# Reordering the beginning of a one-core decoder kernel: loads, transposes, norm factors, constants and masks

## The chip, the cores and the metric

The kernel runs on one core of one Trainium2 chip. The metric is device time in microseconds (us) of one execution. Engines: PE is TensorE, DVE is VectorE, ACT is ScalarE, POOL is GpSimd, SP is SyncE, whose queue issues all DMAs here.

## The reference

One step of a two-layer decoder trunk over 576 tokens: 512 of a prompt and 64 of eight sampled sequences, 1024 features each. Layer A normalises the tokens, multiplies by a weight of 1024 x 8192 and runs a gated recurrence per head; layer B is sliding-window attention. The change touches only the way into layer A:

```python
def rms_norm(x, g):
    xf = x.astype(F32)
    y = xf * lax.rsqrt(jnp.mean(xf * xf, axis=-1, keepdims=True) + EPS)
    return (y * g.astype(F32)).astype(x.dtype)
...
def hgrn2_layer(x, s0, w_in, w_out, g_norm, g_onorm, lb):
    q, fz, i, gate = jnp.split(rms_norm(x, g_norm) @ w_in, 4, axis=-1)
```

## The kernel before

Activations lie with features on the 128 partitions: hT holds 8 feature blocks (k) of 576 tokens. Matrix products keep f32 accuracy by splitting each operand into a rounded part (hi) and the rest (lo) and adding three products: hi x hi, lo of x with hi of w, hi of x with lo of w. A product over all 576 tokens is two halves (j) of HN = 288 tokens, each with 24 steps: 8 k for each of the three terms (`product`, L222 to L236).

Where the tokens come from. `load_tokens` (L154) loads five tiles xt: four of 128 prompt tokens, one of 64 sample tokens. `arrive(i)` (L266 to L284) handles one tile: ScalarE squares it and sums over features (L272); TensorE transposes its eight blocks into two small PSUM tiles px (L276), which VectorE copies to hT (L277); ScalarE forms (mean + eps) to the power of minus one half by Ln and Exp (L278, L279); VectorE multiplies the identity by it (dg, L281); TensorE multiplies ones by dg (pr, L283), which spreads a token's factor over all partitions; ScalarE copies it to rall (L284). pr lies in the pool "m" of two large PSUM tiles that the products pf, pq, pi and pg use as well; px lies in the pool "x" of three.

`normed(j)` (L286 to L293) then makes the operands of one half: for each k, VectorE computes u = hT x gain x rall (L291), ScalarE copies it to xhi (L292), and VectorE, or GpSimd for k in LO_POOL = (1, 4, 7), subtracts to get xlo (L293). The gain is a column of vT, the transpose of a tile vecs that six small loads fill (L175, L298, L299). Half 0 needs tiles 0, 1 and a quarter of tile 2; half 1 needs tiles 2 to 4.

Order as written: loads of tiles 0 to 2, the six small loads, tiles 3 and 4, the sinks (L181); `arrive` of 0, 1, 2; vT; `normed(0)`; `arrive` of 3 and 4; `normed(1)`; the constants of the lower bound (L305 to L325); masks (L327 to L350); then layer A. There, `head_main(0)` (L578) forms pf (weights "a0_1"), pq ("a0_0"), pi ("a0_2") and pg ("a0_3"). Only pf of head 0 takes half 0 before half 1; its pq, pi and pg alternate between halves. `split_weights` (L195) loads a weight of 512 KB (raw, three buffers), casts it on ScalarE (whi, L200) and subtracts on VectorE (wlo, L204; two buffers each).

A scheduler reorders the program: each engine keeps one queue and works through it strictly in order, and the queue is built before the run from the program's order (earlier first), from priorities (`high_priority(offset)` lifts instructions by that many places, BOOST is 800, `early` 100), and from when the scheduler thinks an operand or a buffer is ready. `issue_after(ins)` puts the instructions traced inside it behind `ins` in the queue of the engine of `ins`, and binds no other engine.

## Time and profile before

| | us |
|---|---|
| median of 3 runs | 1169.92 (1169.79 to 1174.06) |
| the profiled execution, own time | 1169.39 |
| its span, first to last instruction | 1167.6 |
| TensorE busy in the span | 1111.7 (95%) |
| VectorE busy | 895.4 (77%) |
| ScalarE busy | 702.1 (60%) |
| GpSimd busy | 340.7 (29%) |

The span is the time between the first and the last instruction in the trace; 1.8 us of the execution's own time lie outside it. Busy time counts instructions of the engine itself; a wait in a queue shows as idle time, and the trace names what ended it. Times in the rows below count from the start of the span.

### The profile page before, as it was taken

Reading aid. Unit: us, or ns where it says so; the run is one execution under the profiler, and the core shown is the slowest. Engines: PE = TensorE matmul, PEld = TensorE weight load, DVE = VectorE, ACT = ScalarE, POOL = GpSimd, SP = SyncE. Lnnn points to the kernel's source line nnn. Section 1 sums busy time; section 2 is a strip of 40 time slices with the busy share of each in tenths; the row PEclk is TensorE's granted clock in tenths of the full one; section 3 lists DMA queues with packets and bytes.
Section 4 is the critical chain, followed back from the end, with each engine's and each line's share of the span. In section 5 each row is a group of like instructions: output and inputs, shape, how many; then the busy total and the mean of one; then the engine's idle time right before and its main releaser. Section 6 shows DMA issues by size and latency. Waiting matters only on the chain.

```text
span 1167.6 us, 27339 instructions
## 1 busy us (share of the span) xinstructions
PE 1111.7 (95%) x10937; PEld 1078.1 (92%) x10937; DVE 895.4 (77%) x2090; ACT 702.1 (60%) x1700; POOL 340.7 (29%) x311
## 2 busy tenths in 40 slices
PE   5999999999999999999999987999999999999997
PEld 5999999999999999999999987989989999999986
DVE  8898776489984597893897779567787778777686
ACT  6776764466662567772767455557655764765545
POOL 1122221112121131110122155444543453454430
PEclk8999999999999999999999998989999999999999
DMA  5332233232332523332232332211212213112102
GB/s 154 100 112 86 84 109 112 59 110 76 110 117 66 147 74 113 97 107 74 76 111 77 103 91 74 68 55 56 73 39 71 74 55 91 56 55 73 56 19 82
DMA packets 161097, 98.01 MB, mean 84 GB/s; under 512 B 3897, under 2 KB 157546, under 8 KB 160938
## 3 DMA queue, kind: packets, MB, share of 16 engines
q1 hardware_dynamic: 160970, 96.26, 28.0%
q8 instruction: 86, 1.41, 0.5%
q14 instruction: 41, 0.34, 0.1%
HBM read 84.06 MB, written 14.16 MB: 84 GB/s over the span
## 4 chain that ended last, share of the span: by engine, by line
PE 45%; DVE 11%; ACT 6%; issue 2%; POOL 1%; DVEq 0%; ACTq 0%; POOLq 0%
PE pbg L211 7%; PE po L211 7%; PE pbq L211 5%; PE po L228 4%; PE pg L228 3%; PE pf L228 3%; PE pi L228 3%; PE pq L228 2%; PE pkv L211 2%; PE sc L1098 2%; ACT P L1127 1%; PE pav L1181 1%; PE pz L211 1%; DVE QS L1289 1%; PE pa L797 1%
## 5 line engine op out<-in xcount | busy, mean ns | idle before, releaser
L606 POOL TENSOR_TENSOR Xl<-Xl 128x72 f32<-128x72 f32 x80 | 50.3, 659 | 205.9 <-DVE Xl L603 204.7
L638 POOL TENSOR_TENSOR sg<-sg,lg 128x576 f32<-128x576 f32 x16 | 26.3, 1642 | 278.4 <-ACT lg L571 278.4
L200 ACT CAST whi_a<-raw_a 128x1024 fp32r<-128x1024 f32 x64 | 67.1, 1049 | 63.4 <-PE po L228 30.8
L204 DVE TENSOR_TENSOR wlo_a<-raw_a,whi_a 128x1024 fp32r<-128x1024 f32 x64 | 81.8, 1282 | 25.0 <-issue 23.6
L1127 ACT ACTIVATE P<-P,st 128x192 f32<-128x192 f32 (+2 forms) x128 | 54.1, 424 | 68.4 <-DVE st L1122 68.4
L1136 POOL TENSOR_SCALAR P<-P,st 128x192 f32<-128x192 f32 (+1 forms) x64 | 48.6, 769 | 117.9 <-DVE st L1129 99.4
L438 DVE TENSOR_TENSOR hT<-hT,po 128x576 f32<-128x576 f32 x32 | 24.1, 754 | 49.6 <-PE po L228 49.3
L200 ACT CAST whi_o<-raw_o 128x1024 fp32r<-128x1024 f32 x30 | 31.4, 1047 | 30.8 <-PE po L228 25.6
L204 POOL TENSOR_TENSOR wlo_bg<-raw_bg,whi_bg 128x1024 fp32r<-128x1024 f32 x16 | 38.4, 2402 | 35.5 <-ACT whi_bg L200 30.0
L228 PE MATMUL po<-oh,whi_o 128*128 128x288 f32 x256 | 42.8, 302 | 4.4 <-ACT whi_o L200 1.9
L211 PE MATMUL po<-olb,whi_o 128*128 128x288 f32 x224 | 43.0, 306 | 3.8 <-DVE olb L1395 1.9
L211 PE MATMUL po<-ohb,whi_o 128*128 128x288 f32 x224 | 43.6, 311 | 2.4 <-DVE Qs L1294 1.7
L662 POOL TENSOR_TENSOR vb<-vst,bmask 128x512 fp32r<-128x512 f32 x32 | 36.7, 1168 | 26.7 <-DVE vst L658 13.8
L204 POOL TENSOR_TENSOR wlo_bq<-raw_bq,whi_bq 128x1024 fp32r<-128x1024 f32 x16 | 38.8, 2430 | 19.2 <-ACT whi_bq L200 19.1
L228 PEld LDWEIGHTS po<-oh,whi_o 128*128 128x128 f32 x256 | 35.9, 188 | 6.3 <-ACT whi_o L200 2.2
L211 PE MATMUL pbq<-xhi,whi_bq 128*128 128x256 f32 (+1 forms) x256 | 41.4, 305 | 0.0
L211 PE MATMUL po<-ohb,wlo_o 128*128 128x288 f32 x224 | 41.3, 301 | 0.0
L228 PE MATMUL po<-ol,whi_o 128*128 128x288 f32 x256 | 40.5, 294 | 0.0
L211 PE MATMUL pbg<-xhi,whi_bg 128*128 128x288 f32 x256 | 40.5, 300 | 0.0
L228 PE MATMUL po<-oh,wlo_o 128*128 128x288 f32 x256 | 40.4, 294 | 0.0
L211 PE MATMUL pbg<-xhi,wlo_bg 128*128 128x288 f32 x256 | 40.1, 299 | 0.0
L204 POOL TENSOR_TENSOR wlo_o<-raw_o,whi_o 128x1024 fp32r<-128x1024 f32 x14 | 33.6, 2399 | 22.0 <-ACT whi_o L200 20.3
(385 smaller groups left out, 3761.4 us busy)
## 6 DMA issues: line engine op xcount, KB each, us to landing
raw_a<-in_w_in_a_dram SPq DMA_DIRECT2D x64, 512.0 KB
S<-in_state_hgrn_dram SPq DMA_DIRECT2D x32, 256.0 KB
out_dram<-S SPq DMA_DIRECT2D x32, 256.0 KB
raw_o<-in_w_out_a_dram SPq DMA_DIRECT2D x16, 512.0 KB
raw_bq<-in_w_in_b_dram SPq DMA_DIRECT2D x16, 512.0 KB
raw_bg<-in_w_in_b_dram SPq DMA_DIRECT2D x16, 512.0 KB
raw_o<-in_w_out_b_dram SPq DMA_DIRECT2D x16, 512.0 KB
xt<-in_x_prompt_dram SPq DMA_DIRECT2D x4, 512.0 KB
```

Of the source, the lines that this page charges most:

```text
L200: act.copy(hi[:, :n], raw[:, :n])
L204: eng.tensor_tensor(lo[:, r], raw[:, r], hi[:, r].bitcast(F32), ALU.subtract)
L211: pe.matmul(pm[:, : c1 - c0], w[:, k * width + w0 : k * width + w0 + P], x(k)[i][:, c0:c1], start=n == 0, stop=n == len(terms) - 1,)
L228: pe.matmul(pm[:, j, :HN], w[:, k * width + c0 : k * width + c0 + P], x(k, j), start=n == 0 and k == 0, stop=n == 2 and k == nk - 1,)
L438: dve.tensor_add(h2, h2, ps2(pm))
L606: pool.tensor_tensor(X8[:, :, j : j + 1], X8[:, :, j : j + 1], X8[:, :, k : k + 1], ALU.add)
L638: (pool if SGP else dve).tensor_tensor(sg, sg, l, ALU.mult)
L662: pool.tensor_tensor(t, view(vst.bitcast(F32), [[0, 4], [1, P]], off=half * P), view(bmask, [[1, 4], [0, P]]), ALU.mult,)
L797: pe.matmul(pa[32 * j : 32 * j + ns, c, t0 : t0 + nt], keys[:, c * P + s0 : c * P + s0 + ns], queries[:, c * P + t0 : c * P + t0 + nt], st ...
L1098: pe.matmul(sc[:, hf, k0[hf] :], QS[pr][:, 2 * n + hf, :], kk[:, g, ks], start=q == 0, stop=q == 1)
L1127: act.activation(x, x, AF.Exp, bias=st[:, a : a + 1], accum_out=st[:, 8 + a : 9 + a])
L1136: (pool if e == "p" else dve).tensor_scalar(x, x, st[:, 8 + a : 9 + a], None, ALU.mult)
```

## The change

Loads (SP's queue): tiles 0 to 2, the gain norm_a into a tile of its own (vec_a), tiles 3 and 4, then the two weights a0_1 and a0_0, then the other five small loads and the sinks. Transposes: `arrive` keeps only transposes and copies to hT; squares, Ln, Exp, dg, pr and rall move to `factors`, with dg on GpSimd instead of VectorE and pr in the pool "x". Order: three tiles arrive, their factors, the gain's transpose, `normed(0)`; the copies of tiles 3 and 4 stand on VectorE behind the last xlo of half 0 (`first`), and the squares and so on of tiles 3 and 4 on ScalarE behind its last xhi (`first_high`). All xlo of `normed` are on VectorE. The casts of the first two weights get priority, right behind the third rall copy (`third`) and behind `first_high`. pq of head 0 takes half 0 before half 1, as pf does. On VectorE, all of head 0's first part stands behind `first`, and constants and masks stand behind the last xlo of half 1 (`second`).

```diff
-LO_POOL = (1, 4, 7)
...
     for i in range(3):
         load_tokens(i)
+    vec_a = stp.tile([KT, P], F32, name="vec_a")
+    sp.dma_start(vec_a, norm_a.rearrange("o (k p) -> (o k) p", p=P))
+    for i in range(3, 5):
+        load_tokens(i)
+
+    raws = {}
+    for part in (1, 0):
+        src = w_in_a[0, :, part * DI : part * DI + P].rearrange("(k p) c -> p k c", p=P)
+        raws[f"a0_{part}"] = wts.tile([P, 1024], F32, tag="raw", name=f"raw_a0_{part}", bufs=3)
+        sp.dma_start(raws[f"a0_{part}"].rearrange("p (a c) -> p a c", a=KT), src)
...
-        sp.dma_start(vecs[row : row + n, :], ap)
+        sp.dma_start(vecs[row - KT : row - KT + n, :], ap)
...
-    for i in range(3, 5):
-        load_tokens(i)
...
-        act.copy(hi[:, :n], raw[:, :n])
+        with ExitStack() as when:
+            if after:
+                when.enter_context(tc.issue_after(after))
+                when.enter_context(tc.high_priority(offset=BOOST))
+            act.copy(hi[:, :n], raw[:, :n])
...
-        junk = stp.tile([P, D], F32, tag="junk", name=f"junk{i}", bufs=2)
-        act.activation(junk[:n], xt, AF.Square, accum_out=q)
...
+    def factors(i):
+
+        n = P if i < 4 else LS
+        q = ssq[:n, i : i + 1]
+        junk = stp.tile([P, D], F32, tag="junk", name=f"junk{i}", bufs=2)
+        act.activation(junk[:n], xts[i][:n], AF.Square, accum_out=q)
         act.activation(q, q, AF.Ln, bias=eps_c[:n], scale=1.0 / D)
         act.activation(q, q, AF.Exp, scale=-0.5)
         dg = stp.tile([P, P], F32, tag="dg", name=f"dg{i}", bufs=2)
-        dve.tensor_scalar(dg[:n, :n], ident[:n, :n], q, None, ALU.mult)
-        pr = half(f"pr{i}")
+        pool.tensor_scalar(dg[:n, :n], ident[:n, :n], q, None, ALU.mult)
+        pr = misc(f"pr{i}")
         pe.matmul(pr[:, :n], ones[:n, :], dg[:n, :n], start=True, stop=True)
-        act.copy(rall[:, r], pr[:, :n])
+        return act.copy(rall[:, i * P : i * P + n], pr[:, :n]).ins
...
-            act.copy(xhi[:, k, r], u)
-            (pool if k in LO_POOL else dve).tensor_tensor(xlo[:, k, r], u, xhi[:, k, r].bitcast(F32), ALU.subtract)
+            high = act.copy(xhi[:, k, r], u)
+            low = dve.tensor_tensor(xlo[:, k, r], u, xhi[:, k, r].bitcast(F32), ALU.subtract)
+        return low.ins, high.ins
 
     for i in range(3):
         arrive(i)
+    for i in range(3):
+        third = factors(i)
+    pv = misc("pva")
+    pe.transpose(pv[:, :KT], vec_a, ident[:KT, :KT])
+    dve.tensor_copy(vT[:, :KT], pv[:, :KT])
+    first, first_high = normed(0)
+    with tc.issue_after(first):
+        for i in range(3, 5):
+            arrive(i)
+    with tc.issue_after(first_high):
+        for i in range(3, 5):
+            factors(i)
+    second, _ = normed(1)
     pv = misc("pv")
     pe.transpose(pv[:, :64], vecs, ident[:64, :64])
-    dve.tensor_copy(vT, pv[:, :64])
-    normed(0)
-    for i in range(3, 5):
-        arrive(i)
-    normed(1)
+    with tc.issue_after(second):
+        dve.tensor_copy(vT[:, KT:], pv[:, :64])
...
+        after = {(0, 1): third, (0, 0): first_high}.get((h, part))
...
-            yield from product(pq, *w, xview(xhi), xview(xlo))
+            yield from product(pq, *w, xview(xhi), xview(xlo), order=((0, 1),) if h else ((0,), (1,)))
...
-        for _ in head_main(0, st):
-            pass
+        with tc.issue_after(first):
+            for _ in head_main(0, st):
+                pass
...
-                make()
+                with tc.issue_after(second):
+                    make()
```

Left out: the same instructions for constants and masks (L305 to L350), now inside `with tc.issue_after(second):`, and the passing of `after` to `split_weights`.

## Rows read from the trace of the kernel before

**Rows 1.** The page, part 1: busy time of each engine over the whole span

```profile
PE 1111.7 (95%) x10937; PEld 1078.1 (92%) x10937; DVE 895.4 (77%) x2090; ACT 702.1 (60%) x1700; POOL 340.7 (29%) x311
```

**Rows 2.** Waits of TensorE, 0 to 60 us: total, times, longest

```profile
PE pr L283 <- DVE dg L281: 6.8, 1, 6.8
```

**Rows 3.** Stretches: length, busy time (count) by engine, PE clock, DMA share, GB/s

```profile
15.00:20.00 5.00, 0.00 (x1) 0.00 (x0) 5.00 (x11) 3.90 (x9) 1.94 (x2) 0.62 0.31 79
20.00:25.00 5.00, 3.17 (x11) 2.81 (x12) 5.00 (x13) 1.87 (x6) 0.84 (x1) 0.50 0.01 4
30.00:50.00 20.00, 20.00 (x156) 20.00 (x154) 15.67 (x38) 13.70 (x26) 3.81 (x6) 1.00 0.41 119
```

**Rows 4.** Timeline of TensorE, 4 to 38 us: start, length, line, tiles, count

```profile
4.32 1.94 PE L276 MATMUL px<-ident,xt 128*128 128x128 f32 x8 [4.32 <-DMA xt<-in_x_prompt_dram]
...
21.78 1.48 PE L283 MATMUL pr<-dg,ones 128*128 128x128 f32 x4 [6.78 <-DVE dg L281]
23.19 2.29 PE L228 MATMUL pf<-xhi,whi_a 128*128 128x288 f32 x8
...
35.57 2.24 PE L228 MATMUL pq<-xhi,wlo_a 128*128 128x288 f32 x16
37.65 0.55 PE L228 MATMUL pi<-xhi,whi_a 128*128 128x288 f32 x3
```

**Rows 5.** Timeline of VectorE, 14 to 31 us

```profile
14.40 1.80 DVE L291 SCALAR_TENSOR_TENSOR u<-hT,vT,rall 128x288 f32<-128x288 f32 x4
...
17.83 2.33 DVE L291 SCALAR_TENSOR_TENSOR u<-hT,vT,rall 128x288 f32<-128x288 f32 x4
20.09 0.81 DVE L293 TENSOR_TENSOR xlo<-u,xhi 128x288 fp32r<-128x288 f32 x2
...
23.60 1.37 DVE L291 SCALAR_TENSOR_TENSOR u<-hT,vT,rall 128x288 f32<-128x288 f32 x3
...
29.25 0.81 DVE L293 TENSOR_TENSOR xlo<-u,xhi 128x288 fp32r<-128x288 f32 x2
```

**Rows 6.** Timeline of ScalarE, 0 to 40 us

```profile
4.21 1.06 ACT L272 ACTIVATE junk<-xt 128x1024 f32<-128x1024 f32 x1 [2.21 <-DMA xt<-in_x_prompt_dram]
...
5.83 1.04 ACT L272 ACTIVATE junk<-xt 128x1024 f32<-128x1024 f32 x1
...
13.47 0.24 ACT L284 COPY rall<-pr 128x128 f32<-128x128 f32 x1
...
14.09 1.05 ACT L200 CAST whi_a<-raw_a 128x1024 fp32r<-128x1024 f32 x1
```

**Rows 7.** Timeline of SyncE's queue, 0 to 42 us

```profile
5.41 0.36 SPq L157 DMA_DIRECT2D xt<-in_x_prompt_dram  x1
...
8.65 15.46 SPq L198 DMA_DIRECT2D raw_a<-in_w_in_a_dram  x4
```

**Rows 8.** Instructions by line and form, 0 to 40 us: busy us, mean ns, idle before

```profile
L277 DVE COPY hT<-px 128x512 f32<-128x512 f32 x8 | 5.4, 684 | 0.6 <-PE px L276 0.6
L204 DVE TENSOR_TENSOR wlo_a<-raw_a,whi_a 128x1024 fp32r<-128x1024 f32 x4 | 5.3, 1326 | 0.0
...
L338 DVE TENSOR_TENSOR ge<-ti,si 128x128 f32<-128x128 int32 x1 | 0.3, 283 | 0.0
```

**Rows 9.** GpSimd's instructions by line and form, whole span

```profile
L1136 POOL TENSOR_SCALAR P<-P,st 128x128 f32<-128x128 f32 x16 | 10.0, 637 | 23.8 <-DVE st L1129 15.6 <-ACT pT L1227 4.5 <-ACT low L1184 3.7
```

**Rows 10.** Stretches in which TensorE's clock changes, columns as in Rows 3

```profile
21.78:26.20 4.42, 4.37 (x16) 3.98 (x17) 4.42 (x10) 1.88 (x6) 0.92 (x1) 0.50 0.21 61
852.80:855.80 3.00, 1.17 (x10) 1.13 (x10) 2.94 (x4) 0.00 (x0) 1.74 (x1) 1.00 0.02 7
855.90:859.10 3.20, 3.20 (x16) 3.20 (x15) 1.92 (x11) 1.36 (x7) 0.00 (x0) 0.50 0.54 154
```

**Rows 11.** Timeline of VectorE, 50 to 58 us

```profile
51.06 0.75 DVE L738 SCALAR_TENSOR_TENSOR KL<-KL,KQ 128x576 f32<-128x576 f32 x1
```

**Rows 12.** Timeline of TensorE from 57 us: first use of the first head's KL

```profile
57.27 0.22 PE L797 MATMUL pa<-KL 128*32 128x32 f32 x1
```

More of the change, by code (lines that the diff above doesn't have):

```diff
@@ L574, in weights_in @@
         def weights_in(h, part):
+            after = {(0, 1): third, (0, 0): first_high}.get((h, part))
             c = part * DI + h * P
[L576 removed]
+            return split_weights(w_in_a[0, :, c : c + P].rearrange("(k p) c -> p k c", p=P), f"a{h}_{part}", after=after)
         def head_main(h, st):
@@ L970, in yoco_kernel @@
             for make in {5: (prompt_mask,), 6: (sample_mask,), 7: (sink_rows,)}.get(h, ()):
-                make()
+                with tc.issue_after(second):
+                    make()
             st = nxt
```

97 lines of the change are left out of this document (48 added, 49 removed).

## The prediction

> **What bounds the kernel now.** I read the page's busy times first: TensorE works 95% of the span [rows 1], so a change at the beginning is worth what it moves TensorE's own work forward, as long as TensorE stays full behind it. The waits of TensorE come next: up to 60 us one wait stands out, 6.8 us for the diagonal dg at L281 [rows 2]. The stretches show the same hole: no work from 15 to 20 us, 3.17 of the next 5 us at a clock of 0.50, and from 30 to 50 us no idle time at all [rows 3]. So the beginning has one weak place, 15 to 26 us, and whatever is won is won when the product pi of head 0 starts, at 37.65 us [rows 4]; from there on TensorE runs full.
>
> Why the hole? TensorE's queue has the products pr of tiles 3 and 4 (21.78) in front of the first product pf (23.19) [rows 4]. Their dg stands in VectorE's queue behind all of half 0, whose subtraction ends at 20.09 + 0.81 = 20.90 [rows 5]. Half 0 began only at 14.40, because the third rall copy came at 13.47 [rows 6]. Weights are not the cause: the first cast of a weight ran at 14.09 [rows 6], nine us ahead of pf. Half 1 starts at 23.60 and ends at 30.06 (29.25 + 0.81) [rows 5].
>
> **The change part by part.** Paces first. VectorE makes an u in 0.45 us (4 in 1.80) and an xlo in 0.405 (2 in 0.81) [rows 5]: a k costs 0.855, a half of eight 6.84 us. A product step takes 0.13 us (16 from 35.57 to 37.65) [rows 4].
>
> Loads. xt3 was issued only at 5.41 and the first weight at 8.65, behind six small loads [rows 7]. Now three tokens, vec_a, two tokens and both weights go first, and five small loads and snk come behind them. The small ones feed vT's rest and sink_rows only, which now come after half 1: hidden. vec_a's 4 KB land beside xt2, while TensorE is still transposing. Earlier weights gain nothing alone, as the cast at 14.09 already lay ahead of its use; the cast of the first weight is now put right behind the third rall copy, and I take it that its data is there by then (the other case is a rival).
>
> Start of half 0. TensorE transposes from 4.32 at 0.24 us each (8 in 1.94) [rows 4]; 24 of them, now in front of the diagonals, end at 10.1. Three pr products follow; a pr cost 0.74 at the lower clock (1.48 for two) [rows 4], say 0.5 at the upper: 11.6. A rall copy takes 0.24 [rows 6] and a handoff 0.1: half 0 starts at 12.0 instead of 14.40. The vec_a transpose and its copy of eight columns lie beside that copy. VectorE's copies of hT (0.684 each [rows 8]) keep up, since the ten mask instructions and the diagonals no longer stand among them. dg on GpSimd has no row; the nearest, a TENSOR_SCALAR of 128x128, takes 0.637 [rows 9]; the lower end is VectorE's own 0.3 or less. Near the upper end only tile 2's counts, and ScalarE is done with that tile long before TensorE is.
>
> Half 0 on VectorE alone: 12.0 + 6.84 = 18.85. Before, GpSimd did three of the eight subtractions in each half (six, as LO_POOL has three k). That saves VectorE three times 0.405 = 1.2 us a half, but four u beside GpSimd took 2.33 instead of 1.80 [rows 5], which gives half of it back; so removing it costs about 0.7 us a half, which is already in the 6.84. The Trainium skill (GPSIMD Engine Reference, Specifications) says the two engines share SBUF interfaces and contend when a VectorE instruction has two SBUF inputs, as u and xlo have; by it alone the removal would look nearly free, and the trace agrees with 2.33 against 1.80.
>
> Start of half 1. This is the late link. ScalarE finishes the last xhi of half 0 near 18.4, and first_high holds everything for tiles 3 and 4 behind it. Then come the boosted cast of the second weight, 1.05 [rows 6], and two tiles at 1.62 each (4.21 to 5.83) [rows 6]: 22.7. Then dg 0.64, pr 0.5 to 0.74, copy 0.24, handoffs: rall is whole at 24.3. VectorE meanwhile does two copies of 0.684, two of half the columns at some 0.4, and two wlo of 1.33 [rows 8]: 18.85 + 2.2 + 2.7 = 23.7, so it waits 0.6 us. Half 1 runs from 24.3 to 31.15, **1.1 us later than the 30.06 of before**.
>
> TensorE. pr is now drawn from the small PSUM tiles, so pf need not stand behind pr3 and pr4: it starts at about 13.5, and the half-0 steps of pf and pq (48) are done before half 1 has delivered much. They have a wide cover, 13.5 to 26 us, even at the lower clock. What is left behind the last xhi of half 1 (30.7) is the xlo and wlo steps of two products: 32 x 0.13 = 4.2, to 34.9 against 37.65: 2.8 us won.
>
> The clock. Half 1 gives TensorE two xhi steps per 0.855 us, 0.26 us of work: 30% busy for over 4 us. No stretch of before is exactly that; the nearest is 852.8 to 855.8, with 1.17 of 3.00 us busy, after which the clock stood at 0.50 for 3.2 us, 1.2 of 2.4 GHz [rows 10]. The beginning of before cost 4.42 us at 0.50 [rows 10]. At that level a step takes twice as long: 3.2 us of it lose 1.6 us, 4.42 lose 2.2, and none lose 0. I take 1.6, by the nearest row. [...]
>
> Moved behind half 1: vT's copy, ten masks and the lower-bound constants, some 25 small instructions of VectorE. The widest takes 0.283 us [rows 8], so at most 7 us; most are far smaller, I take 4. They must lie beside pf's exponentials. VectorE was idle 20.00 - 15.67 = 4.3 us between 30 and 50 us [rows 3], and the first head's KL ended at 51.81 [rows 11], 5.4 us before TensorE used it [rows 12]. With pf 2 us later (at the lower clock) and pa 1.2 us earlier, 2.2 us of that are left: cost nothing, but not by much.
>
> Sum: 2.8 - 1.6 = **1.2 us won**. The profiled execution took 1169.39 (span 1167.6 and 1.8 around it), the median is 1169.92, 0.5 above; profile to profile 1168.2, as a median **1168.7 us**.
>
> **The rivals.**
> 1. Half 1 does not wait for its factors (ScalarE's squares of tiles 3 and 4 slip in earlier, or the cast of the second weight behind them). Then VectorE alone sets it: 18.85 + 2.2 + 6.84 = 27.9, or 29.2 with a wlo in between, and TensorE, dense at the full clock, ends 4.8 to 6.0 us earlier: 1164 to 1165. For it: VectorE has no idle time from 15 to 25 us today [rows 3]; against it: first_high is a hard order. 0.15.
> 2. Slower: TensorE takes the products as written, pf's half 1 before pq's half 0. It decides if the second weight's wlo, which the program names after half 1, is put behind it on VectorE. Then 64 steps stand behind the last xhi: 30.7 + 8.3 + 1.6 = 40.6, 3.0 later than 37.65: 1172.9. 0.13.
> 3. The loads do not come sooner. ScalarE's cast of the first weight now stands in front of all xhi copies, so a weight landing as late as 14.09 holds them: cast to 15.1, first xhi 15.55, while VectorE has filled its four u by 13.8 and stands for 1.75 us. All of it shifts: 2.8 - 1.75 - 1.6 = -0.55, 1170.5. Against it: the queue held the loads back at 5.41 and later, not the memory [rows 7]. 0.08.
>
> **How the numbers follow.** 0.64 is left for the forecast, which with the clock never falling gives 1167.1 and with 2.2 lost 1169.3. A measurement here tells about 0.5%, 5.9 us, from no change. The range runs from rival 1's early end with a little, 1163.5, to rival 2, 1172.9. Faster by over 0.5% needs the whole of rival 1 and some luck with the order of later work: 0.14. Slower by over 0.5% needs rival 2 with a further loss, such as pa waiting for KL: 0.06. Within 0.5%: 0.80.
>
> **What would show it.** Right: first u at 12, its last xlo near 19, pf at 13 to 14, a VectorE gap before half 1 at 24, pi at 35 to 37, a clock of 0.50 somewhere between 16 and 36 us, TensorE full from 37 on. Wrong: pi before 33 (rival 1), pi after 39 with pf's second half before pq's first (rival 2), ScalarE standing before whi for raw (rival 3), or a span that differs from the shift of pi by more than 2 us, which would mean that the later order changed.

## The result, and the profile after

The changed kernel takes 1174.29 us (median of 20 runs) against 1170.25 before (20 runs): the ratio is 1.0029, 95% interval 1.0020 to 1.0039. That is slower by some 3.4 us (the two medians lie 4.0 apart), within the 0.5% that counts as no change, and above the forecast's range. The profiled execution took 1172.9 with a span of 1171.1 (before 1169.39 and 1167.6), so the two profiles differ by 3.5 us, nearly as much, and can be read against each other.

The page's busy times after the change, to set beside [rows 1]: the engines' work is nearly what it was, TensorE 4 us more.

```profile
PE 1115.6 (95%) x10938; PEld 1080.0 (92%) x10938; DVE 896.2 (77%) x2092; ACT 702.0 (60%) x1700; POOL 340.4 (29%) x310
```

The waits of TensorE up to 70 us (us in total, times, longest), to set beside [rows 2]: the 6.8 us for dg are gone, and three waits stand at the start of pi and behind it that were not there.

```profile
PE pf L241 <- ACT xhi L309: 3.9, 5, 1.1
PE pf L241 <- DVE wlo_a L217: 1.8, 1, 1.8
PE pi L241 <- DVE KQ L592: 1.0, 1, 1.0
PE pa L827 <- issue: 0.8, 1, 0.8
```

**The beginning went as forecast up to half 1.** VectorE's timeline after (start, length, engine, line, operation, tile, count, and in brackets the idle time ahead and what ended it), against [rows 5]:

```profile
11.71 1.38 DVE L308 SCALAR_TENSOR_TENSOR u<-hT,vT,rall 128x288 f32<-128x288 f32 x3
17.63 0.89 DVE L310 TENSOR_TENSOR xlo<-u,xhi 128x288 fp32r<-128x288 f32 x2
21.60 2.35 DVE L217 TENSOR_TENSOR wlo_a<-raw_a,whi_a 128x1024 fp32r<-128x1024 f32 x2
25.53 1.38 DVE L308 SCALAR_TENSOR_TENSOR u<-hT,vT,rall 128x288 f32<-128x288 f32 x3 [1.57 <-ACT rall L301]
31.34 0.89 DVE L310 TENSOR_TENSOR xlo<-u,xhi 128x288 fp32r<-128x288 f32 x2
```

Half 0 starts at 11.71 (forecast 12.0, before 14.40) and ends at 17.63 + 0.89 = 18.52 (forecast 18.85, before 20.90). Half 1 starts at 25.53 (forecast 24.3, before 23.60) and ends at 32.23 (forecast 31.15, before 30.06): 2.2 us later than before, where 1.1 was forecast. These are the ends on VectorE; GpSimd's last xlo of before ended at 30.74. VectorE waited 1.57 us for rall. ScalarE's timeline, GpSimd's, and the view of the tile dg from 20 to 26 us (shortest, median and longest ns) say why:

```profile
21.34 0.33 ACT L296 ACTIVATE ssq<-ssq 128x1 f32<-128x1 f32 x2
24.92 0.57 ACT L301 COPY rall<-pr 128x128 f32<-128x128 f32 x2 [3.25 <-PE pr L300]
```

```profile
10.06 0.60 POOL L298 TENSOR_SCALAR dg<-ident,ssq 128x128 f32<-128x128 f32 x1 [1.47 <-PE pr L300]
21.62 3.14 POOL L298 TENSOR_SCALAR dg<-ident,ssq 128x128 f32<-128x128 f32 x2 [10.96 <-ACT ssq L296]
```

```profile
L298 POOL TENSOR_SCALAR dg<-ident,ssq x2: 437/1580/2722, 21.6 to 24.3; 128x128 f32<-128x128 f32 x1, 64x64 f32<-64x64 f32 x1
```

The factors were ready at 21.67, a us sooner than forecast. But tile 3's dg took 2.72 us on GpSimd, from 21.62 to 24.34, beside VectorE's two wlo that run from 21.60 to 23.95: it ended 0.4 us after them. The dg at 10.06, with no such neighbour, took 0.60, and tile 4's, at 24.3, took 0.44. The Trainium skill (SBUF — State Buffer, Who interferes with whom) calls the pair of ports that VectorE and GpSimd share an exclusive lock, held for a whole instruction, which a VectorE operation with two inputs in SBUF contends for with a GpSimd one that reads SBUF. The trace agrees: 2.72 us against 0.60, and the end just behind wlo's, though dg was held over two instructions and not one.

TensorE's timeline after, against [rows 4] and [rows 12]:

```profile
13.13 1.06 PE L241 MATMUL pf<-xhi,whi_a 128*128 128x288 f32 x3 [0.34 <-ACT xhi L309]
35.36 1.22 PE L241 MATMUL pq<-xhi,wlo_a 128*128 128x288 f32 x8
37.58 0.64 PE L241 MATMUL pi<-xhi,whi_a 128*128 128x288 f32 x3 [1.00 <-DVE KQ L592]
57.30 2.38 PE L241 MATMUL pf<-xhi,wlo_a 128*128 128x288 f32 x16 [1.80 <-DVE wlo_a L217]
64.71 0.19 PE L827 MATMUL pa<-G 128*16 128x16 f32 x1 [0.83 <-issue]
```

pf starts ten us sooner (13.13 against 23.19), and the last step of pq ends at 36.58, 1.2 us before the 37.81 of before: the forecast's gain, to the tenth. There it stops. pi waits a whole us for KQ (VectorE, L592), which reads pq out of one of the two large PSUM tiles and so frees it, and starts at 37.58 against 37.65. VectorE's rows of these reads, after and then before (lf at L625 and L595 is the last to read pf):

```profile
36.68 0.76 DVE L592 TENSOR_SCALAR KQ<-pq 128x576 f32<-128x576 f32 x1 [0.28 <-DMA S<-in_state_hgrn_dram]
39.21 0.75 DVE L625 SCALAR_TENSOR_TENSOR lf<-pf,lf 128x576 f32<-128x576 f32 x1
```

```profile
36.03 0.76 DVE L595 SCALAR_TENSOR_TENSOR lf<-pf,lf 128x576 f32<-128x576 f32 x1
37.85 0.76 DVE L563 TENSOR_SCALAR KQ<-pq 128x576 f32<-128x576 f32 x1 [1.05 <-PE pq L228]
```

Before, pi started ahead of KQ, in the tile that lf had left at 36.79. After, it started ahead of lf, in the tile of pq itself. It could not be free sooner: KQ began 0.1 us behind pq's last step, when VectorE had been idle for 0.28 us, so VectorE was not late for it. The order of pq brings this about. In two halves, pq ends 2.3 us behind pf (34.32 to 36.58); alternating, as before, it ended 5.3 us behind it (32.48 to 37.81), time enough to read pf out.

Then head 1's pf stands for 1.80 us behind its wlo, and a product pa pauses for 0.83 with no operand late that the trace names. In VectorE's queue after:

```profile
53.16 0.75 DVE L592 TENSOR_SCALAR sg<-pg 128x576 f32<-128x576 f32 x1
54.89 1.22 DVE L805 TENSOR_TENSOR KQ<-KQ,E 128x1024 f32<-128x1024 f32 x1
56.03 1.22 DVE L217 TENSOR_TENSOR wlo_a<-raw_a,whi_a 128x1024 fp32r<-128x1024 f32 x1
```

And in the kernel before, VectorE's timeline, then TensorE's, over the same instructions:

```profile
53.40 1.22 DVE L204 TENSOR_TENSOR wlo_a<-raw_a,whi_a 128x1024 fp32r<-128x1024 f32 x1
54.54 0.75 DVE L563 TENSOR_SCALAR sg<-pg 128x576 f32<-128x576 f32 x1
55.20 1.21 DVE L775 TENSOR_TENSOR KQ<-KQ,E 128x1024 f32<-128x1024 f32 x1
```

```profile
55.03 2.29 PE L228 MATMUL pf<-xhi,wlo_a 128*128 128x288 f32 x16
```

Before, wlo stood ahead of sg and KQ, was done at 54.62 and was used at 55.03: 0.4 us of slack. After, the queue has sg and KQ first, and wlo is done at 57.25. Of the 2.63 us by which it starts later, 1.8 are the places of sg and KQ (0.66 and 1.14 us of the queue), and 0.8 is VectorE's own lateness.

**Where the 3.5 us are.** For every profile of this study I took three numbers against the profile of before: how much later pi of head 0 starts, how long TensorE waits behind it up to head 1's pg, and how much later that pg starts. The first two add up to the third within half a us where the granted clock held in that stretch; in e10, e13, e14 and e15 it did not, and the steps themselves took 1.5 to 4.2 us more. After: -0.07 + 1.8 + 0.8 = 2.5, and pg is 2.47 late. The other us comes at 268 to 276 us, where TensorE's stretches (busy time of PE, PEld, DVE, ACT, POOL; PEclk, DMA share, GB/s) after and then before are:

```profile
268.00:272.00 4.00, 2.64 (x30) 1.85 (x29) 3.91 (x8) 3.91 (x8) 0.00 (x0) 1.00 0.00 0
272.00:276.00 4.00, 3.67 (x17) 3.67 (x18) 3.88 (x9) 3.85 (x18) 0.00 (x0) 0.57 0.50 147
```

```profile
268.00:272.00 4.00, 2.96 (x20) 2.58 (x21) 3.88 (x8) 3.94 (x15) 0.00 (x0) 1.00 0.42 125
272.00:276.00 4.00, 4.00 (x31) 3.92 (x30) 4.00 (x10) 3.79 (x13) 0.00 (x0) 1.00 0.10 27
```

In both kernels TensorE has gaps at 268; only after does the granted clock then fall to 0.57, and 16 steps of pi take 3.58 us instead of 2.37 (after, then before):

```profile
272.78 3.58 PE L241 MATMUL pi<-xlo,whi_a 128*128 128x288 f32 x16
```

```profile
270.17 2.37 PE L228 MATMUL pi<-xlo,whi_a 128*128 128x288 f32 x16
```

The lateness grows there from 2.42 to 3.80 us; by the end of the kernel it is 3.5. Other profiles have such a dip at other places or not at all.

### The profile page after: what moved, and what is told of

It reads as the page before. It is cut to its first block, busy times and chain, and to the rows that moved or that the text cites. A ratio compares the mean times of both kernels' runs of the same rounds, so it can differ in the third digit from the quotient of the medians.

```text
span 1171.1 us, 27350 instructions
## 1 busy us (share of the span) xinstructions
PE 1115.6 (95%) x10938; PEld 1080.0 (92%) x10938; DVE 896.2 (77%) x2092; ACT 702.0 (60%) x1700; POOL 340.4 (29%) x310
## 4 chain that ended last, share of the span: by engine, by line
PE 46%; DVE 11%; ACT 5%; issue 2%; POOL 1%; DVEq 0%; ACTq 0%; POOLq 0%
PE pbg L224 7%; PE po L224 6%; PE pbq L224 5%; PE po L241 4%; PE pg L241 3%; PE pf L241 3%; PE pi L241 3%; PE pq L241 2%; PE pkv L224 2%; PE sc L1130 2%; ACT P L1159 1%; PE pav L1213 1%; PE pz L224 1%; PE pa L827 1%; DVE QS L1321 1%
## 5 line engine op out<-in xcount | busy, mean ns | idle before, releaser
L241 PE MATMUL pf<-xhi,whi_a 128*128 128x288 f32 x256 | 41.5, 306 | 4.0 <-ACT xhi L309 3.9
L241 PEld LDWEIGHTS pf<-xhi,whi_a 128*128 128x128 f32 x256 | 35.4, 189 | 6.4 <-ACT xhi L309 5.6
L241 PE MATMUL pf<-xhi,wlo_a 128*128 128x288 f32 x256 | 37.6, 298 | 3.7 <-DVE wlo_a L217 3.7
```

Source lines behind the costliest of these rows:

```text
L241: pe.matmul(pm[:, j, :HN], w[:, k * width + c0 : k * width + c0 + P], x(k, j), start=n == 0 and k == 0, stop=n == 2 and k == nk - 1,)
```

## The experiments

The letters in the expectations: A, the place of that one wlo in VectorE's queue; B, masks and constants behind half 1; C, half 1's end, carried along VectorE's chain to head 0's attention copy; D, the forecast's rule that only the start of pi counts; E, a loss made only by the order behind 50 us, which pq's order in halves upsets; F and H, the amount of VectorE's work; G, late factors passed on through pf. A shift is against the profile of before; a ratio is to the runs of before on the same chip, 1.0029 being that of the change. Executions differ at the front even where nothing there was edited: half 1 ends 0.73 us late in e13 and 0.69 in e16, whose edits lie behind it. A shift of less than a us tells little.

**e1: lift the late wlo (from after).**

```diff
-                eng.tensor_tensor(lo[:, r], raw[:, r], ...
+                with tc.high_priority(offset=BOOST if name == "a1_1" else 0):
+                    eng.tensor_tensor(lo[:, r], raw[:, r], ...
```

> The changed kernel, with only the subtraction for head 1's first weight (wlo of a1_1) lifted in VectorE's queue, so that it stands some fifteen places earlier. Theory A (the late place of that one subtraction costs TensorE its 1.8 us wait at 55.5 us): the wait goes, product pi of head 1 starts near 69 instead of 70.8, and the time falls by 1.5 to 2.5 us. Rival B (VectorE simply has too much work between 32 and 57 us, the masks and constants among it): the same work in another order, so the wait moves to the products pa of head 0 and the time stays within 0.7 us.

1175.73 us, 1.0042 (1.0029 to 1.0055). The lifted wlo ran at 45.57 and the wait for it is gone. But kd, Qz and the wlo behind them now ran beside GpSimd's vb and sg (57.40 to 61.47) and took 1.26, 1.06 and 2.48 us instead of 0.42, 0.22 and 1.22; TensorE waited further on, for kt and for S:

```profile
PE pu L874 <- ACT kt L861: 1.6, 1, 1.6
```

A's fall of 1.5 to 2.5 us did not come. As the new place of that wlo cost VectorE some 2.9 us elsewhere, the run does not tell what the wait alone was worth.

**e2: masks back ahead of half 1 (from after).** The lower-bound constants stay behind it.

```diff
-    with tc.issue_after(second):
-        m_ge, m_8 = ...
+    m_ge, m_8 = ...
...
-                with tc.issue_after(second):
-                    make()
+                make()
```

> The changed kernel, with the ten mask instructions and the sinks no longer bound behind half 1; they run among the first copies of hT, as before the change. Rival B (moved work crowds VectorE): 2 us of VectorE work leave the stretch from 32 to 57 us, the 1.8 us wait for wlo of head 1 goes, and the time falls by about 2 us. Theory A (order, not amount): the wait for that wlo stays, because the subtraction still stands behind KQ, and the time changes by less than 1 us.

1177.58 us, 1.0058 (1.0045 to 1.0071): worse. One of the mask instructions, at the head of VectorE's queue, needed an iota that stood on GpSimd behind two dg, and VectorE stood 2.76 us for it (e10 shows such a row). That held the hT copies, so that the first u came at 14.66 and half 1 ended 5.1 us late. pi starts 2.90 late, the waits for wlo and at pa are there as well (1.7 and 1.8), sum 6.4, pg 6.28. The wait for wlo stays though the masks are gone from behind half 1, which speaks against B. The time decides nothing, as the held copies made half 1 late.

**e3: factors of tiles 3 and 4 not held behind the last xhi (from after).**

```diff
-    with tc.issue_after(first_high):
-        for i in range(3, 5):
-            factors(i)
+    for i in range(3, 5):
+        factors(i)
```

> The changed kernel, with the squares and factors of tiles 3 and 4 not bound behind the last xhi of half 0. Theory C (the late rall holds half 1, and with it pf, back): half 1 starts near 23 instead of 25.5, pf's last step comes 2 us earlier than 34.3, pi at 35.5 to 36.5 instead of 37.6, and the time falls by 1 to 2 us if the rest keeps its order. Rival D (pi's start is set by when a PSUM tile comes free): half 1 is earlier, pi is not, and the time stays within 0.7 us.

1172.92 us, 1.0017 (1.0005 to 1.0029). The edit did not bring half 1 forward: on ScalarE the squares of tiles 3 and 4 (9.28 to 12.57) now stood ahead of the rall copies, so half 0 began at 14.24. Half 1 ends 3.2 us late and pi starts 2.87 late, but nothing waits behind it, and pg is 2.68 late, as in after. A kernel that is late at pi ends no later than one that is on time there: with pi so late, the wlo that stands behind sg and KQ here too is in time.

**e4: head 0's pq alternating between halves, as before (from after).**

```diff
-            yield from product(pq, ..., order=((0, 1),) if h else ((0,), (1,)))
+            yield from product(pq, ...)
```

> The changed kernel, with head 0's pq alternating between the halves as before the change. Rival E (the split of pq into halves upsets the order behind it): the time falls by 2 to 3 us. Theory A: in VectorE's queue head 1's wlo stands ahead of sg and KQ again, as before the change, so the 1.8 us wait goes; but 16 more steps stand behind the last xhi of half 1, so pi starts about 1 us later (38.5) and the time falls by 0.5 to 1.5 us.

1171.54 us, 1.0009 (0.9999 to 1.0019). By the ratios that is 2.3 us below after, the 2 to 3 us that E had forecast. All three waits of after are gone, and in VectorE's queue wlo is ahead of sg (and of KQ, at 57.62) again, as A and E had it:

```profile
55.81 1.22 DVE L217 TENSOR_TENSOR wlo_a<-raw_a,whi_a 128x1024 fp32r<-128x1024 f32 x1
56.95 0.75 DVE L592 TENSOR_SCALAR sg<-pg 128x576 f32<-128x576 f32 x1
```

pi is 2.88 late and pg 2.42, with no wait between them. The profiled execution took 1173.83 us, 2.3 above the median of the run: ScalarE stood 0.91 us for the first weight, and half 1 ended 4.1 us late, 1.9 later than in after. Even so pg is no later than in after. So the 1.2 us that the order in halves won at pq was lost again behind it.

**e5: pr from the small PSUM tiles alone (from before).**

```diff
-        pr = half(f"pr{i}")
+        pr = misc(f"pr{i}")
```

> Edit of the kernel before, one line: pr of the five tiles is drawn from the small PSUM tiles, as the change does, so that pf of head 0 need not stand behind pr of tiles 3 and 4 on TensorE. Nothing of VectorE, ScalarE or GpSimd moves. Theory C (VectorE's queue sets the time from the end of half 1, 30.1 us in the profile of before, to head 0's copy att at 62.1 us): pf starts some 5 us earlier (near 17 instead of 23.2), half 1 still ends within 0.5 us of 30.1, att's copy comes within 0.7 us of 62.1, and the time is that of before within 1 us. Rival D (TensorE is full from 30 us on, so an earlier product start is worth its whole length, the rule of the forecast): pi of head 0 starts 2 to 4 us earlier and the time falls by as much.

1170.16 us, 0.9995 (0.9985 to 1.0004). pf starts at 17.06 instead of 23.19, and pi 0.22 later than before, with half 1 ending 1.27 later (31.33). The one wait of 6.8 us that I had put first was worth nothing that shows in the time: xlo and wlo steps wait for half 1 in any case.

**e6: VectorE held up ahead of half 1 (from before),** by four fills of a tile that nothing reads.

```diff
-    normed(0)
+    first = normed(0)
+    idle = stp.tile([P, 576], F32, name="idle")
+    with tc.issue_after(first):
+        with tc.high_priority(offset=BOOST):
+            for i in range(4):
+                dve.memset(idle, float(i))
```

> Edit of the kernel before: four memsets of a 128x576 tile that nobody reads, about 0.5 us each by the widest copies of this size, some 2.2 us together, stand on VectorE behind the last subtraction of half 0 and ahead of half 1. Everything else is as before. Theory C: half 1 ends 2.2 us later, near 32.3 (where the change puts it), head 0's copy att comes 2.2 us later, near 64.2, and the time rises by 2 us or a little more, to 1172 to 1174. Rival D (VectorE has 4.3 us idle between 30 and 50 us and 5.4 us of slack at KL, as the forecast priced it): att's copy moves by less than 1 us, and the time stays within 1 us of before, or follows pi's start alone.

1171.89 us, 1.0011 (1.0002 to 1.0020). Half 1 ends 1.75 late, pi starts 2.38 and pg 1.84 late: a late half 1 costs, in before as well, here some 1.3 us.

**e7: dg of tiles 3 and 4 on VectorE (from after).**

```diff
-        pool.tensor_scalar(dg[:n, :n], ...
+        (dve if i > 2 else pool).tensor_scalar(dg[:n, :n], ...
```

> Edit of the changed kernel: the diagonals dg of tiles 3 and 4 are made on VectorE, as in the kernel before, and no longer on GpSimd, where the two took 1.5 us each beside VectorE's wlo. Theory C: dg takes 0.3 us, rall is whole some 1.2 us sooner if dg's place in VectorE's queue is ahead of wlo (near 23.7), half 1 ends near 31 instead of 32.2, and the time is 1 to 1.3 us below the changed kernel's, between it and before; if dg stands behind the two wlo, nothing is won. Rival E (the loss lies only in the order behind 50 us, whenever half 1 ends): half 1 ends earlier and the time stays the changed kernel's within 0.7 us.

1173.49 us, 1.0025 (1.0015 to 1.0034): the same as after. The two dg are short now (0.44 for both), but without a lift they stood behind a wlo in VectorE's queue, at 23.47, behind an hT copy that came at 22.00; half 1 began at 26.20. To be held by wlo in the queue or beside it on GpSimd came to the same.

**e8: factors of tiles 3 and 4 between the xhi copies of half 0, and e4 (from after).**

```diff
+            if not j and k in (2, 5):
+                with tc.issue_after(high.ins):
+                    with tc.high_priority(offset=BOOST):
+                        factors(3 + k // 5)
```

> Edit of the changed kernel: the factors of tiles 3 and 4 are put on ScalarE between the xhi copies of half 0 (behind its third and its sixth), no longer behind the last one, and head 0's pq takes its steps in the two halves alternately, as in the kernel before. Theory C: half 0 runs at most 2 us longer on VectorE (its u wait for ScalarE's copies), half 1 follows behind the hT copies without a wait for rall and ends between 29 and 30.5 us, 2 to 3 us sooner than in the changed kernel; head 0's copy att comes as much earlier as half 1 ends, and the time is at or up to 1 us below before, 1169 to 1171.5. Rival F (the masks and constants that were moved behind half 1 are what costs, about 2 us of VectorE wherever half 1 ends): half 1 ends sooner, and att's copy and the time stay 1.5 us or more above before.

1174.70 us, 1.0032 (1.0018 to 1.0046). The factors were early, but the hT copies of tiles 3 and 4 then waited 3.4 us for their transposes behind TensorE's steps; half 1 ran from 26.94 to 34.53, and pi is 2.82 late. Tiles 3 and 4 need both.

**e9: three xlo of each half on GpSimd again (from after).**

```diff
-            low = dve.tensor_tensor(xlo[:, k, r], ...
+            low = (pool if k in (1, 4, 7) else dve).tensor_tensor(xlo[:, k, r], ...
```

> Edit of the changed kernel: three of the eight xlo subtractions of each half go back to GpSimd (k = 1, 4, 7), as in the kernel before. It takes 6 x 0.405 = 2.4 us of instructions off VectorE, and gives about half of it back, as u beside GpSimd is slower. Theory G (half 1's start is held by its factors, and behind half 1 the chain through pf, ka and the scan sets the time, not the volume of VectorE's work): half 0 ends at most 1 us sooner, half 1 still starts within 0.5 us of 25.5 and ends within 0.5 us of 32.2, and the time is the changed kernel's within 1 us. Rival H (VectorE's volume of work ahead of head 0's att copy, some 53.5 us in every run, sets that copy; the moved subtractions are what costs): att's copy and the time come 1.5 to 2.4 us sooner.

1174.69 us, 1.0031 (1.0019 to 1.0043). Half 1 ends at 33.01 on VectorE, later than 32.23, but the first weight came 1.2 us later too (ScalarE stood 1.27 us for it, 0.19 in after). H gets no support: fewer instructions for VectorE gained nothing, as three u beside GpSimd take 1.90 us instead of 1.38.

**e10: fills to GpSimd behind its last dg, masks first (from after).**

```diff
-    with tc.issue_after(second):
-        m_ge, m_8 = ...
+    m_ge, m_8 = ...
...
-        dve.memset(rmask, 1.0)
+        with tc.issue_after(dgs[-1]):
+            pool.memset(rmask, 1.0)
```

> Edit of the changed kernel: the fourteen memsets that fill VectorE from 1.8 to 5.0 us go to GpSimd, behind its last dg, and the nine mask instructions take their place on VectorE ahead of the first hT copy. Behind half 1 VectorE has only the twelve small instructions of the lower bounds left. The front up to half 1's end does not move (within 0.4 us). Rival H (volume): about 1.8 us of VectorE's work are gone from the 32 us behind half 1, so att's copy and the time come 1.5 to 1.8 us sooner. Theory G (chain through pf): the mask instructions stood beside pf's last steps and ScalarE's first exponentials, so what is won is at most the delay of ka, 0.5 us, and the time falls by 0.5 us or less.

1177.18 us, 1.0059 (1.0038 to 1.0081). The fault of e2 again: the mask operations stood at the head of VectorE's queue, and one of them needed the iota behind two dg:

```profile
8.64 0.17 DVE L379 TENSOR_SCALAR bi<-bi 128x4 int32<-128x4 int32 x1 [6.07 <-POOL bi L378]
```

First u at 14.80, half 1 done at 35.36, pi 3.07 late. A tiny instruction on an ordered queue held everything by 3 us.

**e11: e10, e8 and the hT copies of tiles 3 and 4 not held (from after).**

```diff
-    with tc.issue_after(first):
-        for i in range(3, 5):
-            arrive(i)
+    for i in range(3, 5):
+        arrive(i)
```

> Edit of the changed kernel, a version meant to beat both: masks first and memsets on GpSimd (as e10), squares of tiles 3 and 4 between the xhi copies of half 0 and pq's steps alternating (as e8), and the hT copies of tiles 3 and 4 no longer held behind half 0, with the weight's wlo ahead of them. By every theory half 0 starts near 11.7, and TensorE's transposes no longer hold VectorE as in e8 (3.4 us there). If half 1 then ends by 31 us, theory C gives att's copy at 62 to 62.5 us and a time of 1169.5 to 1171; with rival H's 1.8 us for the masks on top 1168 to 1169. If half 1 ends at 32 us or later again, only the masks' part is left: 1171 to 1173.

1179.49 us, 1.0070 (1.0053 to 1.0086): both faults together, half 1 done at 38.22, pi 6.31 late and pg 6.23.

**e12: fills on GpSimd and masks first in the kernel before.** The fills go to GpSimd as in e10, held behind nothing; the two large iotas and the six mask instructions that use them are lifted by BOOST, bmask's three are not.

> Edit of the kernel before: the fourteen memsets go from VectorE to GpSimd and five of the mask instructions, with the high priority of the weights' casts, into VectorE's stretch from 1.7 to 4 us that they leave; nothing else is changed. The hT copies start about 0.8 us sooner than 8.64. Theory C (what VectorE's start and half 1's end move by, the time moves by): first u 0.6 to 1 us sooner than 14.40, half 1 ends 0.5 to 1 us sooner than 30.06, att's copy and the time 0.5 to 1 us less. Rival D (TensorE's product start alone counts): the time follows pi's start. If neither half 1's end nor pi moves, the third rall copy on ScalarE (13.47) held the front, and the time stays within 0.5 us of before.

1170.97 us, 0.9998 (0.9986 to 1.0009), pi 0.58 sooner. No effect that can be measured.

**e13: head 1's wlo late, and nothing else (from before),** by four fills of 128x192, of a tile that is not written yet, behind head 0's E.

```diff
+            if not h:
+                with tc.issue_after(last.ins):
+                    with tc.high_priority(offset=BOOST):
+                        for i in range(4):
+                            dve.memset(amask, float(i))
```

> Edit of the kernel before: four memsets of a 128x192 tile that is not used yet, some 0.7 us, stand on VectorE behind head 0's E (53.0 us), and by them VectorE's queue gets the order of the changed kernel there: sg and the long KQ ahead of the wlo of head 1's first weight. Up to 53 us nothing moves, half 1 and TensorE's start of pi included. Theory C (the wlo has 55.03 - 54.62 = 0.4 us of slack, and what it is later beyond that TensorE waits): the wlo ends at 57 us, TensorE waits about 2 us for it, and the products behind come 1.8 to 2.2 us later, the time by as much, less what the KQ that now comes earlier gives back. Rival D (the products' start sets the time, and VectorE's slack is the 5.4 us of KL): pi does not move and the time stays within 0.7 us of before.

1173.34 us, 1.0015 (1.0006 to 1.0023). VectorE's queue took the order of after, from an added 0.9 us of work, and TensorE's timeline and the stretches (columns as above) show what follows:

```profile
54.92 0.69 DVE L563 TENSOR_SCALAR sg<-pg 128x576 f32<-128x576 f32 x1
55.74 1.16 DVE L780 TENSOR_TENSOR KQ<-KQ,E 128x1024 f32<-128x1024 f32 x1
56.82 1.21 DVE L204 TENSOR_TENSOR wlo_a<-raw_a,whi_a 128x1024 fp32r<-128x1024 f32 x1
```

```profile
58.08 3.89 PE L228 MATMUL pf<-xhi,wlo_a 128*128 128x288 f32 x16 [2.16 <-DVE wlo_a L204]
```

```profile
55.80:58.10 2.30, 0.14 (x2) 0.02 (x1) 2.27 (x4) 2.25 (x6) 0.00 (x0) 1.00 0.00 0
58.10:60.10 2.00, 2.00 (x10) 2.00 (x11) 1.96 (x3) 1.05 (x2) 1.91 (x2) 0.60 0.21 63
```

This is the wait of after made in before, with half 1 nearly on time: 2.2 us lost, and 1.5 more as the clock fell to 0.60 after the standstill and the 16 steps took 3.89 us (2.38 in after, which kept the full clock). The profile is 4.12 us late at pg (0.73 + 2.2 + 1.5 = 4.4), and its execution took 1174.30, the longest of the eleven. The median rose by 1.8 us, half of the change's loss. So a late wlo costs by itself, and 0.4 us of slack is all that stood against it.

**e14: both wlo of pi and pg of head 0 on GpSimd (from after).**

```diff
-        c = n * share[0] // 8
+        c = 0 if name in ("a0_2", "a0_3") else n * share[0] // 8
```

> Edit of the changed kernel: two wlo subtractions of head 0 (the weights of pi and pg, 1.22 us each on VectorE, at 34.4 and 38.1 us) go to GpSimd, which has nothing to do between 25 and 43 us. Theory C: VectorE's chain through pf, the scan and E comes 1 to 2.4 us sooner (the small constants and KQ wait no longer behind them), so that TensorE's wait of 1.8 us for the wlo of head 1 shrinks below 0.8 us, and the time falls by 1 to 2.4 us towards before. If GpSimd's wlo takes more than 2.5 us each, pi or pg waits for it instead and eats part of that. Rival D: pi's start unmoved, time within 0.7 us of the changed kernel.

1177.20 us, 1.0052 (1.0039 to 1.0066). VectorE's load went down and its time went up. GpSimd's row, and two of VectorE's beside it:

```profile
34.40 4.75 POOL L217 TENSOR_TENSOR wlo_a<-raw_a,whi_a 128x1024 fp32r<-128x1024 f32 x2 [9.70 <-ACT lnlb L354]
```

```profile
34.43 2.40 DVE L357 TENSOR_TENSOR lnlb<-lnlb,lbe 128x16 f32<-128x16 f32 x1
36.84 2.34 DVE L432 COPY snk<-snk 64x16 f32<-64x16 f32 x1
```

Two instructions of 16 columns, 0.17 us otherwise, took 2.4 each, one for each wlo, and pi then waited 3.9 us for KQ.

**e15: e14, and dg of tiles 3 and 4 lifted on VectorE.**

```diff
-        pool.tensor_scalar(dg[:n, :n], ...
+        with tc.high_priority(offset=BOOST if i > 2 else 0):
+            (dve if i > 2 else pool).tensor_scalar(dg[:n, :n], ...
```

> Edit of the changed kernel: as e14, and the diagonals dg of tiles 3 and 4 on VectorE with the high priority of the weights' casts, so that they stand behind the first wlo and ahead of the second. Half 1 then starts near 24.2 instead of 25.5 and ends near 30.9 instead of 32.2. Theory C: both gains add, head 0's chain comes 2.3 to 3.7 us sooner than in the changed kernel, TensorE waits for no wlo, and the time is 1169.5 to 1171.5, at or a little below before. If the time is that of e14, what is won at half 1 is lost again to a wait further on, and this run's waits name it.

1177.97 us, 1.0057 (1.0045 to 1.0069). The block of e14 again; in this profile ScalarE's first whi also stood 2.13 us for its weight's load.

**e16: e14's edit in the kernel before.**

> Edit of the kernel before, the control for e14: the same two wlo subtractions on GpSimd. Theory C with TensorE as the bound in the kernel before (no wait of TensorE between 26 and 57 us for VectorE): nothing is won, the time stays within 0.7 us of before; VectorE's idle time grows instead. If the time falls by 1 us or more, VectorE was a bound in the kernel before too, and the two kernels do not differ in what bounds them.

1173.29 us, 1.0020 (1.0008 to 1.0032): the block costs there too, with pi 1.11 and pg 2.36 late.

**e17: half 1 sooner in every link (from after):** factors of tiles 3 and 4 lifted, their dg on VectorE, their transposes and copies not held, pq alternating.

```diff
-    with tc.issue_after(first):
-        for i in range(3, 5):
-            arrive(i)
+    for i in range(3, 5):
+        arrive(i)
     with tc.issue_after(first_high):
-        for i in range(3, 5):
-            factors(i)
+        with tc.high_priority(offset=2 * BOOST):
+            for i in range(3, 5):
+                factors(i)
...
```

> Edit of the changed kernel, meant to keep its gain: factors of tiles 3 and 4 with twice the priority of the weights' casts (their squares stand ahead of the second weight's cast on ScalarE, their pr ahead of pf's and pq's later steps on TensorE), their dg on VectorE, their transposes no longer held behind half 0, and head 0's pq in alternating steps as before. VectorE's queue behind 50 us then has the order of the kernel before: wlo ahead of sg and KQ. Half 1 starts near 23.5 and ends near 30 (the changed kernel 25.5 and 32.2). Theory C (half 1's end sets pi's start and VectorE's chain, and nothing is lost behind it as the wlo is in time): pi near 36.5, some 1 us before the kernel before, no wait of TensorE at 55 us, no pause in the scores, and a time of 1169.5 to 1171, 0 to 1.5 us below before. Rival H (the masks behind half 1 are in VectorE's way): the wlo is 1 to 2 us late again and the time 1 us or more above before.

1169.99 us, **0.9982 (0.9972 to 0.9993)**: below before by more than the interval, though within the 0.5% as well. Half 1 runs from 24.42 to 31.12, a us sooner than after. Head 1's wlo (54.20) is back ahead of sg (55.34) and KQ (56.00), and from 24 to 80 us TensorE waits for nothing but xhi. The edit holds e4's: that alone is at 1.0009, and with half 1 sooner as well the time is 0.9982, some 3 us less. No run has half 1 sooner with pq in halves. ScalarE's and VectorE's rows show the chain:

```profile
22.32 0.20 ACT L296 ACTIVATE ssq<-ssq 64x1 f32<-64x1 f32 x1
23.77 0.61 ACT L301 COPY rall<-pr 128x128 f32<-128x128 f32 x2 [1.26 <-PE pr L300]
```

```profile
22.10 0.28 DVE L298 TENSOR_SCALAR dg<-ident,ssq 128x128 f32<-128x128 f32 x1
22.62 0.25 DVE L298 TENSOR_SCALAR dg<-ident,ssq 64x64 f32<-64x64 f32 x1 [0.24 <-ACT ssq L296]
24.42 1.38 DVE L308 SCALAR_TENSOR_TENSOR u<-hT,vT,rall 128x288 f32<-128x288 f32 x3 [0.42 <-ACT rall L301]
```

**e18: e17, with masks first, the iota lifted and the fills on GpSimd behind the third dg.**

> Edit of the changed kernel: as e17, and the nine mask instructions ahead of the first hT copy on VectorE, in the place of the fourteen memsets, which go to GpSimd behind its third dg; the small index that held VectorE in e10 is made first on GpSimd. Theory C: the front is that of e17 (first u 11.5 to 12, half 1's end near 30), the masks are off the path behind half 1, head 0's chain comes up to 1 us sooner than in e17, and as TensorE then is the bound, the time is e17's or up to 0.5 us below it. Rival H: 1.5 to 2 us below e17.

1169.88 us, **0.9981 (0.9969 to 0.9993)**. First u 11.43, half 1 from 23.90 to 30.59, pi 0.73 sooner than before, TensorE's waits from 24 to 70 us 0.3 in all. In VectorE's queue at head 1's pf, wlo (52.23) is ahead of sg (53.37) and KQ (54.04).

Both variants are about 2 us below before and some 5 below the change as it stands (0.9981 and 0.9982 against 1.0029). Their intervals overlap, so what the masks add is not told apart: with the iota in time, masks ahead of half 1 cost nothing that shows, and neither do masks behind it.

**All together**, shifts against the profile of before, in us:

| | pq of head 0 | half 1's end | pi, head 0 | pg, head 1 | profiled execution | ratio |
|---|---|---|---|---|---|---|
| e12 | alternating | -0.6 | -0.6 | -0.6 | -0.3 | 0.9998 |
| e18 | alternating | +0.5 | -0.7 | -1.1 | -0.9 | 0.9981 |
| e16 | alternating | +0.7 | +1.1 | +2.4 | +2.2 | 1.0020 |
| e13 | alternating | +0.7 | +0.7 | +4.1 | +4.9 | 1.0015 |
| e17 | alternating | +1.1 | +1.3 | +0.9 | +1.1 | 0.9982 |
| e5 | alternating | +1.3 | +0.2 | -0.3 | +1.6 | 0.9995 |
| e6 | alternating | +1.8 | +2.4 | +1.8 | +3.4 | 1.0011 |
| e4 | alternating | +4.1 | +2.9 | +2.4 | +4.4 | 1.0009 |
| e8 | alternating | +4.5 | +2.8 | +2.7 | +6.2 | 1.0032 |
| e11 | alternating | +8.2 | +6.3 | +6.2 | +10.0 | 1.0070 |
| e14 | in halves | +2.1 | +2.8 | +8.2 | +10.0 | 1.0052 |
| after | in halves | +2.2 | -0.1 | +2.5 | +3.5 | 1.0029 |
| e7 | in halves | +2.8 | +0.5 | +3.0 | +4.2 | 1.0025 |
| e1 | in halves | +2.9 | +0.7 | +4.3 | +4.9 | 1.0042 |
| e9 | in halves | +3.0 | +0.9 | +3.7 | +4.4 | 1.0031 |
| e3 | in halves | +3.2 | +2.9 | +2.7 | +2.4 | 1.0017 |
| e15 | in halves | +3.7 | +4.3 | +7.3 | +8.5 | 1.0057 |
| e2 | in halves | +5.1 | +2.9 | +6.3 | +8.0 | 1.0058 |
| e10 | in halves | +5.3 | +3.1 | +6.3 | +7.6 | 1.0059 |

Two groups stand out. Where pq alternates, head 1's pg follows the start of pi within 0.6 us: there the forecast's rule D holds, and C with it, as pi itself comes later with a later half 1. The exceptions are e13, which makes the wlo late, and e16, with GpSimd's wlo. Where pq runs in halves, pg comes 2.4 us and more later than pi would have it, e3 alone excepted. There wlo stands behind sg in VectorE's queue (e1 lifts it out of there), and pi waits for a tile: 0.9 to 1.0 us in six of the nine, 0.5 in e3, 3.9 in e14 and e15. In the alternating ones wlo stands ahead of sg everywhere but in e13, and pi waits 0 to 0.4 us.

One profile stands for each kernel, and it need not be like the median: that of e4 is 4.4 us above the profile of before, its ratio 1 us above the runs of before. Behind head 1's pg the profiles lose up to 3.8 us more (e11), which is not taken apart.

## Why the prediction was wrong

**Right:** half 0's start and end, the time of pf, and the end of pq (1.2 us won, as the sum had it, though by luck: see the clock).

**The step that failed** is the sentence that from pi on TensorE runs full, so that what is won at the end of pq is won for good, and with it that one slack, the 5.4 us at KL, stands for all that VectorE feeds behind pi. (KL itself was in time: done at 48.36, used at 59.63.) The 2.8 us of the sum count 32 steps behind half 1's last xhi instead of the 48 that an alternating pq would leave: 2.1 us of them (16 x 0.13) are the order of pq, priced by its steps alone. What that order does behind pq was not looked at. pf now ends only 2.3 us ahead of pq, so pi has to take pq's own tile and waits 1.0 us until KQ has read it. And the queue, built anew, has sg and KQ ahead of head 1's wlo, which had 0.4 us of slack: 1.8 us, and 0.8 more at pa. That is 3.6 us against 2.1. e4 takes back that one line and nothing else: the three waits are gone, and the loss falls from 3.4 us to 1.1 (1.0009, whose interval includes no change). e13 makes the wait for wlo alone in the kernel before, and it costs.

The rest is half 1, which is late. e17 and e18, which alternate pq and have half 1 a us and more sooner than after, beat both kernels. I had measured one slack, the largest, at one consumer. The forecast's own list of signs has this case as its last one, a span that differs from the shift of pi: the shift is -0.07, the span 3.5.

**A term that was mis-sized:** dg on GpSimd, taken as 0.64 us from [rows 9]. Tile 3's took 2.72 beside VectorE's wlo, four times the upper bound. That bound came from a row without such a neighbour, though the forecast had priced the contention of u by [rows 5] a few lines earlier. rall was whole at 25.49 instead of 24.3, and half 1 was late by 2.2 instead of 1.1. With half 1's measured end in the sum the forecast would still have had 0.1 us won, far from 3.4 us lost: this term is the smaller part of the miss. (The masks that it counted as ten are nine in the trace, which changes nothing.)

**The clock:** the 1.6 us were put between half 1 and pi. After shows 0.50 up to 22.9 and the full clock from there on, also from 26 to 36, while half 1's products trickle in. TensorE was busy 8.39 of those 10 us, not the 30% on which the term rested: the half-0 steps that pf and pq still had filled the gaps.

```profile
16.50:22.90 6.40, 5.47 (x22) 4.71 (x22) 5.12 (x11) 4.50 (x11) 1.28 (x1) 0.50 0.00 0
26.00:36.00 10.00, 8.39 (x57) 7.53 (x57) 9.87 (x39) 6.35 (x15) 0.00 (x0) 1.00 0.30 85
```

The end of pq came out right by luck: half 1 was 1.1 us later and the clock term 1.6 us smaller than forecast, and the two nearly cancel. And the clock cost 1.4 us where I had not looked, at 272 us.

**The rivals:** 1 did not come about: half 1 waited. 2's order did not either (pq's half 0 ran before half 1), but its price of 3 us on the slow side was nearly what another mechanism took. 3 hardly did in this profile, where ScalarE stood 0.19 us for the first weight. But it stood 0.3 to 1.3 us in e1, e4, e7, e8, e9, e14, e17 and e18 and 2.13 us in e15, with the same order of loads, so part of what sets these kernels apart may be that.

**Open:** the pause at pa, which the trace puts down to no operand: 0.7 to 0.8 us in e7, e9 and after, 1.5 to 1.8 in e14, e15 and e2, and none where pq alternates; why the order of pq changes VectorE's queue twenty us behind it; why the clock dips near 270 us in some profiles and not in others. No run took these apart, and none has pq in halves in the kernel before.

## What to carry to other kernels

Where TensorE is full, a gain at the beginning counts only as far as every engine that feeds it is sooner too: list the slack of each operand and of each PSUM tile for the next head or two, and take the smallest, not the one that looks like the cover. An order that ends two products close together leaves the third without a free tile. A scheduler that builds static queues reorders work far behind the edit, so read its order at those thin places before believing that a time shift passes through unchanged. Take a change that bundles several edits back one by one: here one line of it made some 2 of the 3.4 us. When a step goes to GpSimd, price it with what VectorE will run beside it, and hold the whole chain to its consumer together (e7 and e8 mended one or two links and won nothing; e17 mended all).

## What the runs showed of the hardware that was not expected

A GpSimd TENSOR_TENSOR of 128x1024 held VectorE instructions of 16 columns for its whole 2.4 us (e14: 2.40 and 2.34 instead of 0.17); two wlo of VectorE held a dg of 0.60 us on GpSimd for 2.72, so either engine can be the one that stands. Fills did not do it: in e18 GpSimd filled tiles at 10.3 to 13.4 us while three u took 1.38 us, as in after without them. And the same standstill of TensorE was followed by either clock. In after and e9 it waited 1.80 and 2.17 us for wlo, the granted clock stayed at 1.00, and the 16 steps behind took 2.38 and 2.39 us. In e10 and e13 it waited 1.80 and 2.16 us in the same place, the clock fell to 0.60, and the same steps took 3.89 us. What decides between the two is not shown. TensorE's rows in e9, then in e10:

```profile
58.65 2.39 PE L241 MATMUL pf<-xhi,wlo_a 128*128 128x288 f32 x16 [2.17 <-DVE wlo_a L217]
```

```profile
60.45 3.89 PE L241 MATMUL pf<-xhi,wlo_a 128*128 128x288 f32 x16 [1.80 <-DVE wlo_a L217]
```
